# A three-branch decoder trunk: the first loads on two queues, the first piece reordered, the roots spread in two parts, the output in three pieces

## The chip, the core and the metric

The kernel runs on one core of one Trainium2 chip. Its time is what the device measures from the start to the end of one execution, in microseconds; a run's figure is the median of several executions. TensorE is called PE here, VectorE DVE, ScalarE ACT, GpSimd POOL and SyncE SP. SP does nothing here but issue transfers; ACT and POOL issue some too.

## The reference

Two layers (`DEPTH` 2) work on 256 tokens of width 1024, all in float32. Each layer normalises the stream, multiplies it by one wide matrix, feeds three token mixers, gates and adds their projections, and adds the result to the stream. A last normalisation ends the trunk.

```python
for layer in range(DEPTH):
    h = rms_norm(x, norm_w[layer])
    proj = jnp.einsum('bsd,de->bse', h, w_in[layer])       # 1024 -> 12,832 columns
    (a_xbc, a_z, a_dt, b_q, b_k, b_v, b_z,
     c_q, c_k, c_v, c_f, c_z, gates) = jnp.split(proj, split_at, axis=-1)
    y_a = mamba2_branch(...)            # state space scan
    y_b = sliding_window_branch(...)    # windowed attention with sinks
    y_c = forgetting_attention_branch(...)
    branch = jnp.einsum('bsiw,iwd->bsid', jnp.stack([y_a, y_b, y_c], axis=2), w_proj[layer])
    g = jax.nn.sigmoid(gates.reshape(b, s, 3, d) + gate_bias[layer])
    x = x + jnp.einsum('bsd,de->bse', jnp.sum(g * branch, axis=2), w_out[layer])
return rms_norm(x, final_norm_w)
```

`rms_norm` multiplies a token by the inverse root of its mean square, and each channel by a weight.

## The kernel before

**Products in three parts.** A float32 matrix is split in a high part, which has the short format that PE multiplies in one pass, and a low part, the rest. A product is high x high, low x high and high x low (`hh`, `lh`, `hl`; the letter of the tokens comes first). ACT makes the high part by a copy (`hi`), DVE the low part by a subtraction with two inputs in SBUF (`lo`).

**Weights in pieces and parts.** The weights are taken in pieces of 256 or 512 columns. A piece comes in parts of 512 KB: four blocks of 128 rows where it has 256 columns, two where it has 512. `load_part` issues the transfers of a part, and the part with number 0 comes in two halves of 256 KB. Six raw buffers (`N_RAW`) let the first six parts be asked for ahead. After these a load waits until its buffer has been split.

**The order.** In the first stage (`tc.manual_schedule` over PE, DVE, ACT and POOL) the order of each of these four engines is the order of the lines. Then only PE's order is that of the lines, and a scheduler places the other engines' work. Every engine takes its own instructions strictly in their order: an instruction that waits holds up all behind it.

**The start, line by line.** The norm weights come by ACT's queue (L183). ACT loads its function table for Exp (L186). SP's queue brings the first 128 tokens in two halves (L189), then the first weight part in two halves and the second part (L363), the second 128 tokens (L1416), the third part, the rope table (L1418), and three more parts. While PE waits it runs transposes of an identity (`WARM`, `FILL`). Then:

- `turn(t, j)` transposes half j of token block t on PE (L113), and DVE multiplies it by the norm weights (L1440) into `xw`;
- `high(t, j)` and `low(t, j)` split it (L1444, L1448);
- `w_high(part, i)` and `w_low(part, i)` split half i of a weight part (L1453, L1459);
- `hh`, `lh`, `hl` multiply four blocks of rows at a time for one token block: all of the first piece, 48 products of 256 columns (L109);
- `square(t, j)` takes sums of squares of the tokens on ACT (L244).

The tokens of the first three pieces are multiplied without their roots: the inverse roots `y0.rn` (`root` on POOL, L227, `rsqrt` on DVE, L234 to L238) are applied when ACT evicts the results (L536, L1028). The `late` list holds the evictions of the first piece.

**The normalising product.** `normalize` spreads the roots over the partitions: ACT writes a diagonal matrix for each token block (L1386), PE multiplies it by ones in plain float32, and DVE multiplies `xw` by what comes out (L1396). This product stands in PE's order after the second piece and ahead of the third. The pieces from then on:

```python
op(v, *(u_bv(y, t, first) for t in range(2)))            # first piece: multiplied already
op(None, lambda: layer_consts(y0, nc.gpsimd))
op(None, lambda: launch(9, normalize(y0), 0.0))
op(cv0, u_cv(y, 0, 0), u_cv(y, 0, 1))                    # second piece
op(cv1, u_cv(y, 256, 0), u_cv(y, 256, 1))                # third piece
```

**The end.** `out_end` adds the residual, takes sums of squares and the root for each token block, multiplies 640 columns on DVE and 384 on ACT, and sends them by SP's and ACT's queues (L1219 to L1222).

Of the kernel before, what the change touches and what calls it, by code (L numbers as in the profile page):

```python
# [14 lines left out]
ALU = mybir.AluOpType  # L15
# [20 lines left out]
FILL = 10  # L36
# [14 lines left out]
def hybrid_trunk(  # L51
# [134 lines left out]
    act(tab, tab, AF.Exp)  # L186
# [167 lines left out]
    def load_part(j):  # L354
# [5 lines left out]
        for c, ap in src:  # L360
            m = ap.shape[-1]
            for h in range(0, kper, step_):
                nc.sync.dma_start(raw[:, h:h + step_, c:c + m],  # L363
                                  ap.rearrange("(k p) c -> p k c", p=P)[:, k + h:k + h + step_, :])
# [828 lines left out]
    def out_end(y, c, t, i, n, xo, p):  # L1193
        sl = slice(c, c + n)
        with tc.high_priority():
# [19 lines left out]
            if i == 2:  # L1215
                r = row_rsqrt2(v, last)
                if last:
                    m = 640
                    ts(y.xn[:, t, 0:m], y.xn[:, t, 0:m], r[:, 0:1], None, op0=ALU.mult)  # L1219
                    nc.sync.dma_start(out2[t * P:(t + 1) * P, 0:m], y.xn[:, t, 0:m])  # L1220
                    act(y.xn[:, t, m:D], y.xn[:, t, m:D], AF.Copy, scale=r[:, 0:1])  # L1221
                    nc.scalar.dma_start(out2[t * P:(t + 1) * P, m:D], y.xn[:, t, m:D])  # L1222
# [159 lines left out]
    def normalize(y):  # L1382

        rb = T("L1", [P, S])
        for t in range(2):
            act(rb[:, t * P:(t + 1) * P], ident, AF.Copy, scale=y.rn[:, t:t + 1])  # L1386
        yield 2.0
        p = pmx()
        for t in range(2):
            mm(p[:, t * P:(t + 1) * P], ones, rb[:, t * P:(t + 1) * P], start=True, stop=True)  # L1390
# [23 lines left out]
    with tc.manual_schedule(engines={ENG.PE, ENG.DVE, ENG.Activation, ENG.Pool}):  # L1414
        load_to(2)
        nc.sync.dma_start(x0[:, 1, :], x2[P:S, :])  # L1416
        rope_sb = fin["rope"] = T("L1", [P, 2, 2, 64])
        nc.sync.dma_start(rope_sb, rope_tab.rearrange("(t p) c d -> p t c d", p=P))  # L1418
        load_to(N_RAW)
# [35 lines left out]
        def w_low(part, i):  # L1455
# [3 lines left out]
            tt(lo[:, ks, :], raw[:, ks, :], hi[:, ks, :].bitcast(F32), op=ALU.subtract)  # L1459
# [7 lines left out]
        def keys(t, k0, a, b, ends=False):  # L1467

            for k in range(k0, k0 + 4):
# [5 lines left out]
        def hh(t, k0):  # L1475
            keys(t, k0, y0.hTh, w0.hi)

        def lh(t, k0):
            keys(t, k0, y0.hTl, w0.hi)

        def hl(t, k0):
            keys(t, k0, y0.hTh, w0.lo, True)

        square(0, 0)
        turn(0, 0)
        high(0, 0)
        w_high(parts[0], 0)
# [3 lines left out]
        low(0, 0)  # L1491
        w_high(parts[0], 1)
        high(0, 1)
        w_low(parts[0], 0)
        w_low(parts[0], 1)
        w_high(parts[1], 0)
        w_high(parts[1], 1)
        low(0, 1)
        w_low(parts[1], 0)
        w_low(parts[1], 1)  # L1500
        hh(0, 0)
        lh(0, 0)
        hl(0, 0)
        hh(0, 4)
# [73 lines left out]
```

## Time and profile before

| | us |
|---|---|
| median of 3 runs | 808.71 (808.34 to 808.9) |
| the profiled execution's own time | 808.15 |
| its span, first to last instruction | 806.4 |
| PE busy | 796.9 |
| DVE busy | 684.6 |
| ACT busy | 534.0 |
| POOL busy | 171.6 |
| mean granted clock of PE | 0.999 |

The span leaves out 1.7 us around it. In a row of the timeline stand start and length in us, the engine, the line, the operation, what it writes and reads, the shapes and how many; in brackets stands how long the engine had idled before, and for what. A row of several can show overlapping instructions, so its length is not their sum. `mx` and `mm` are PSUM buffers, `L` stands for several kinds of tile, and `raw`, `hi` and `lo` for weights as loaded, their high parts and their low parts.

### The profile page before, as it was taken

The page shows a single profiled execution, that of the slowest core. Times are in us where ns is not written, and L with a number is a line of the kernel's source. Part 1 is how long each engine was busy: PE and PEld are TensorE (multiplying, and loading weights), DVE is VectorE, ACT ScalarE, POOL GpSimd, SP SyncE. Part 2 cuts the span into 40 slices and gives each one's busy share as a digit, 9 for nine tenths or more (in the row PEclk, how much of TensorE's full clock was granted, in tenths as well). Part 3 has the DMA queues.
Part 4 walks back from the last instruction along what each step waited for, and adds up shares of the span by engine and source line. Part 5 has one row for each costly group of instructions (what it writes and reads, how often), then busy time and mean ns, then how long its engine had stood idle before and what let it go on. Part 6 is the DMA issues. An engine that isn't in the chain of part 4 may idle for free.

```text
span 806.4 us, 14834 instructions
## 1 busy us (share of the span) xinstructions
PE 796.9 (99%) x5162; PEld 710.7 (88%) x5162; DVE 684.6 (85%) x1414; ACT 534.0 (66%) x1144; POOL 171.6 (21%) x238
## 2 busy tenths in 40 slices
PE   8999999999999999999999999999999999999996
PEld 7998988888888888888999899888889988888896
DVE  6869999998899997795785799999879999869865
ACT  7777767875775785543665678677747768845452
POOL 3166113130320100133001741122312120012000
PEclk9999999999999999999999999999999999999999
DMA  9998888797665566686678987679986656576632
GB/s 313 279 261 177 243 223 200 214 294 221 172 203 172 162 195 195 199 254 205 217 245 259 235 212 217 160 216 284 264 230 185 192 150 184 173 235 220 210 107 77
DMA packets 138826, 170.43 MB, mean 211 GB/s; under 512 B 9352, under 2 KB 106464, under 8 KB 138752
## 3 DMA queue, kind: packets, MB, share of 16 engines
q1 hardware_dynamic: 114960, 140.53, 56.4%
q0 software_dynamic: 13328, 13.29, 10.2%
q10 hardware_dynamic: 10464, 15.67, 6.6%
q8 instruction: 41, 0.67, 0.3%
q14 instruction: 33, 0.27, 0.1%
HBM read 154.71 MB, written 2.16 MB: 195 GB/s over the span
## 4 chain that ended last, share of the span: by engine, by line
PE 97%; DVE 1%; DMA 1%; issue 0%; ACT 0%; SPq 0%; DVEq 0%
PE mm L109 84%; PE mx L109 10%; PE mx L113 3%; DMA raw<-in_w_in_dram 1%; DVE lo L294 0%; DVE L L1097 0%; SPq L363 0%; SPq L189 0%; DVE L L1440 0%; ACT L L1444 0%; ACT hi L1453 0%; ACT L L1221 0%; DVE L L1196 0%; DVE L L1200 0%; DVE L L288 0%
## 5 line engine op out<-in xcount | busy, mean ns | idle before, releaser
L109 PE MATMUL mm<-L,hi 128*128 128x512 f32 x1056 | 354.0, 387 | 0.7 <-DVE L L1097 0.7
L294 DVE TENSOR_TENSOR lo<-raw,hi 128x1024 fp32r<-128x1024 f32 (+1 forms) x276 | 312.2, 1150 | 44.0 <-ACT hi L293 42.6
L293 ACT ACTIVATE hi<-raw 128x1024 fp32r<-128x1024 f32 (+1 forms) x276 | 265.8, 982 | 58.3 <-PE mm L109 45.2
L109 PE MATMUL mm<-hi,L 128*128 128x512 f32 (+2 forms) x1168 | 303.4, 349 | 0.1
L109 PE MATMUL mm<-L,lo 128*128 128x256 f32 x1056 | 266.6, 273 | 0.0
L109 PEld LDWEIGHTS mm<-hi,L 128*128 128x128 f32 x1168 | 205.7, 190 | 23.1 <-issue 1.7
L109 PEld LDWEIGHTS mm<-L,hi 128*128 128x128 f32 x1056 | 194.9, 190 | 27.3 <-issue 5.5
L109 PEld LDWEIGHTS mm<-L,lo 128*128 128x128 f32 x1056 | 202.1, 191 | 5.4
L109 PE MATMUL mm<-lo,L 128*128 128x512 f32 (+2 forms) x584 | 201.5, 347 | 0.0
L109 PEld LDWEIGHTS mm<-lo,L 128*128 128x128 f32 x584 | 110.2, 190 | 10.7
L491 POOL DMA_DIRECT2D L<-L x68 | 60.1, 908 | 192.8 <-ACT L L490 165.1
L1066 POOL TENSOR_SCALAR_AFFINE_SELECT bias<-bias 128x128 f32<-128x128 f32 x64 | 33.7, 559 | 76.9 <-DMA bias<-cumd 76.7
L831 DVE SCALAR_TENSOR_TENSOR L<-L,vec,L 128x255 f32<-128x255 f32 (+2 forms) x96 | 46.2, 481 | 2.0 <-ACT L L828 0.3
L489 ACT ACTIVATE L<-mm 128x256 f32<-128x256 f32 x84 | 31.8, 379 | 19.2 <-PE mm L109 14.4
L655 ACT ACTIVATE pp<-pp,nm 128x128 f32<-128x128 f32 x64 | 28.2, 442 | 23.8 <-DVE nm L649 23.8
L1100 ACT ACTIVATE L<-L 128x512 f32<-128x512 f32 x24 | 15.2, 631 | 31.4 <-DVE L L1097 27.0
L491 POOL DMA_DIRECT2D qt<-L x16 | 13.8, 860 | 76.4 <-ACT qt L490 76.4
L613 ACT ACTIVATE pp<-pp,nm 128x128 f32<-128x128 f32 x32 | 12.6, 394 | 25.6 <-DVE nm L618 24.8
L978 POOL TENSOR_TENSOR sm<-sm,mhalf 128x8 f32<-128x8 f32 x2 | 5.2, 2593 | 111.6 <-DVE sm L976 111.6
L490 ACT ACTIVATE L<-mm 128x256 f32<-128x256 f32 x68 | 26.1, 383 | 1.2 <-DMA L<-L 1.2
L1097 DVE TENSOR_TENSOR L<-mm,L 128x512 f32<-128x512 f32 x22 | 15.1, 686 | 13.6 <-PE mm L109 12.1
L1133 POOL TENSOR_TENSOR L<-L,L 128x512 f32<-128x512 f32 x8 | 12.8, 1603 | 55.4 <-DVE L L1132 49.8
(212 smaller groups left out, 925.1 us busy)
## 6 DMA issues: line engine op xcount, KB each, us to landing
raw<-in_w_in_dram SPq DMA_DIRECT2D x191, 512.0 KB, 5.1
raw<-in_w_proj_dram SPq DMA_DIRECT2D x48, 512.0 KB, 5.9
L<-L POOLq DMA_DIRECT2D x72, 128.0 KB, 5.4
raw<-in_w_out_dram SPq DMA_DIRECT2D x16, 512.0 KB, 5.2
bias<-cumd ACTq DMA_DIRECT2D x16, 256.0 KB, 3.3
L<-cumd ACTq DMA_DIRECT2D x8, 512.0 KB, 6.3
L<-in_gate_bias_dram ACTq DMA_DIRECT2D x12, 256.0 KB, 6.2
qt<-L POOLq DMA_DIRECT2D x16, 128.0 KB, 6.0
```

The lines of the kernel that those rows point to most:

```text
L109: nc.tensor.matmul(o, a, b, **kw)
L113: nc.tensor.transpose(o, a, i)
L293: keep(act)(hi, src, AF.Copy)
L294: keep(tt)(lo, src, hi.bitcast(F32), op=ALU.subtract)
L489: act(halves(lo), ordered(p[:, S:2 * S]), AF.Copy)
L490: last = act(halves(out), ordered(p[:, 0:S]), AF.Copy)
L491: nc.gpsimd.dma_start(out, lo, accum_op=ALU.add)
L655: act(pp[:, i, sl], pp[:, i, sl], AF.Exp, scale=-1.0, bias=nm[:, e:e + 1], accum_out=sums[:, e:e + 1])
L831: stt(a[:, s:S], x_[:, 0:S - s], y.vec[:, 16 * j + u:16 * j + u + 1], a[:, s:S], op0=ALU.mult, op1=ALU.add)
L1066: nc.gpsimd.affine_select(out=bias[:, i, dst], in_=bias[:, i, src], compare_op=ALU.is_ge, fill=NEG, base=0, pattern=[[-1, P]], channel_mul ...
L1097: tt(halves(g), p, halves(y.gb), op=ALU.add)
L1100: finish(act(g, g, AF.Tanh, scale=0.5))
```

## The change

- The first two weight parts go by ACT's queue. SP's queue has the tokens, then the other parts, then the rope table. The table load for Exp stands behind ACT's issues.
- In the first stage weights and tokens are split in another order, and the products of the first piece are taken in another order, some two blocks at a time. The low half of the second weight part is made by POOL (`gtt`) in place of DVE. There are three filling transposes in place of ten.
- Sums of squares come later on ACT: the second behind the split of the third part, and the last two behind the split of the fourth.
- `normalize` writes the roots as a high part (ACT) and a low part (DVE), and multiplies both by ones in the one-pass format: two products of 256 columns in place of two in plain float32.
- The evictions of the first piece come in reverse order.
- The output of each token block goes in three pieces: 352 and 352 columns by DVE and SP's queue, 320 by ACT and its queue.

```diff
@@ -33,7 +33,7 @@
 N_RAW, N_SPLIT = 6, 6
 AHEAD = 4
 WARM = 7
-FILL = 10
+FILL = 3
 D_ADD = 6.0
 EARLY = 4
 MEET = 5.0
@@ -183,7 +183,6 @@
     nc.scalar.dma_start(nw8, norm_w[0:1, :].rearrange("o (k p) -> (o k) p", p=P))
     tab = T("tab", [P, 1])
     nc.vector.memset(tab, 0.0)
-    act(tab, tab, AF.Exp)
     x0 = T("L8", [P, 2, D])
     for j in range(2):
         nc.sync.dma_start(x0[:, 0, j * 512:(j + 1) * 512], x2[0:P, j * 512:(j + 1) * 512])
@@ -360,7 +359,7 @@
         for c, ap in src:
             m = ap.shape[-1]
             for h in range(0, kper, step_):
-                nc.sync.dma_start(raw[:, h:h + step_, c:c + m],
+                (nc.scalar if j < 2 else nc.sync).dma_start(raw[:, h:h + step_, c:c + m],
                                   ap.rearrange("(k p) c -> p k c", p=P)[:, k + h:k + h + step_, :])
         raws[j] = raw
 
@@ -1215,11 +1214,13 @@
             if i == 2:
                 r = row_rsqrt2(v, last)
                 if last:
-                    m = 640
-                    ts(y.xn[:, t, 0:m], y.xn[:, t, 0:m], r[:, 0:1], None, op0=ALU.mult)
-                    nc.sync.dma_start(out2[t * P:(t + 1) * P, 0:m], y.xn[:, t, 0:m])
-                    act(y.xn[:, t, m:D], y.xn[:, t, m:D], AF.Copy, scale=r[:, 0:1])
-                    nc.scalar.dma_start(out2[t * P:(t + 1) * P, m:D], y.xn[:, t, m:D])
+                    for a, b in ((0, 352), (352, 704), (704, D)):
+                        o = y.xn[:, t, a:b]
+                        if b < D:
+                            ts(o, o, r[:, 0:1], None, op0=ALU.mult)
+                        else:
+                            act(o, o, AF.Copy, scale=r[:, 0:1])
+                        (nc.sync if b < D else nc.scalar).dma_start(out2[t * P:(t + 1) * P, a:b], o)
                 else:
                     h = layers[y.l + 1].h[t] = T("L4", [P, D])
                     for j in range(2):
@@ -1381,13 +1382,15 @@
 
     def normalize(y):
 
-        rb = T("L1", [P, S])
+        rb = [T("L1", [P, S], F32R) for _ in range(2)]
         for t in range(2):
-            act(rb[:, t * P:(t + 1) * P], ident, AF.Copy, scale=y.rn[:, t:t + 1])
+            h, l = (r[:, t * P:(t + 1) * P] for r in rb)
+            act(h, ident, AF.Copy, scale=y.rn[:, t:t + 1])
+            stt(l, ident, y.rn[:, t:t + 1], h.bitcast(F32), op0=ALU.mult, op1=ALU.subtract)
         yield 2.0
         p = pmx()
-        for t in range(2):
-            mm(p[:, t * P:(t + 1) * P], ones, rb[:, t * P:(t + 1) * P], start=True, stop=True)
+        for i in range(2):
+            mm(p[:, 0:S], onesr, rb[i], start=(i == 0), stop=(i == 1))
         both_streams(y)
         hTh, hTl = y.normal
         for k in (0, 4):
@@ -1413,10 +1416,11 @@
     ENG = mybir.EngineType
     with tc.manual_schedule(engines={ENG.PE, ENG.DVE, ENG.Activation, ENG.Pool}):
         load_to(2)
+        act(tab, tab, AF.Exp)
         nc.sync.dma_start(x0[:, 1, :], x2[P:S, :])
+        load_to(N_RAW)
         rope_sb = fin["rope"] = T("L1", [P, 2, 2, 64])
         nc.sync.dma_start(rope_sb, rope_tab.rearrange("(t p) c d -> p t c d", p=P))
-        load_to(N_RAW)
         warm = pmx()
         for i in range(WARM):
             transpose(warm[:, 0:P], ident, ident)
@@ -1452,11 +1456,11 @@
             m = raw.shape[1] // 2
             act(hi[:, i * m:i * m + m, :], raw[:, i * m:i * m + m, :], AF.Copy)
 
-        def w_low(part, i):
+        def w_low(part, i, f=tt):
             raw, hi, lo = part
             m = raw.shape[1] // 2
             ks = slice(i * m, i * m + m)
-            tt(lo[:, ks, :], raw[:, ks, :], hi[:, ks, :].bitcast(F32), op=ALU.subtract)
+            f(lo[:, ks, :], raw[:, ks, :], hi[:, ks, :].bitcast(F32), op=ALU.subtract)
 
         def square(t, j):
             sum_sq(x0, t, 512 * j, ss[:, 2 * t + j:2 * t + j + 1], 512)
@@ -1464,62 +1468,70 @@
         parts = [new_part() for _ in range(4)]
         first.extend((pmx(), pmm()))
 
-        def keys(t, k0, a, b, ends=False):
-
-            for k in range(k0, k0 + 4):
+        def keys(t, k0, n, a, b, ends=False):
+
+            for k in range(k0, k0 + n):
                 mm(first[t][:, 0:256], a[:, t, k, :], in_turn(b(k)),
                    start=(k == 0 and a is y0.hTh and not ends), stop=(k == NK - 1 and ends))
 
         w0 = pieces[0]
 
-        def hh(t, k0):
-            keys(t, k0, y0.hTh, w0.hi)
-
-        def lh(t, k0):
-            keys(t, k0, y0.hTl, w0.hi)
-
-        def hl(t, k0):
-            keys(t, k0, y0.hTh, w0.lo, True)
+        def hh(t, k0, n=4):
+            keys(t, k0, n, y0.hTh, w0.hi)
+
+        def lh(t, k0, n=4):
+            keys(t, k0, n, y0.hTl, w0.hi)
+
+        def hl(t, k0, n=4):
+            keys(t, k0, n, y0.hTh, w0.lo, True)
 
         square(0, 0)
         turn(0, 0)
+        w_high(parts[0], 0)
+        w_low(parts[0], 0)
         high(0, 0)
-        w_high(parts[0], 0)
+        low(0, 0)
         turn(0, 1)
         for i in range(FILL):
             transpose(warm[:, 0:P], ident, ident)
-        low(0, 0)
         w_high(parts[0], 1)
+        w_low(parts[0], 1)
         high(0, 1)
-        w_low(parts[0], 0)
-        w_low(parts[0], 1)
-        w_high(parts[1], 0)
-        w_high(parts[1], 1)
         low(0, 1)
-        w_low(parts[1], 0)
-        w_low(parts[1], 1)
-        hh(0, 0)
-        lh(0, 0)
-        hl(0, 0)
-        hh(0, 4)
+        hh(0, 0, 2)
+        hl(0, 0, 2)
+        lh(0, 0, 2)
+        hh(0, 2, 2)
+        lh(0, 2, 2)
+        hl(0, 2, 2)
         turn(1, 0)
         turn(1, 1)
-        lh(0, 4)
-        square(0, 1)
+        w_high(parts[1], 0)
+        w_low(parts[1], 0, gtt)
         high(1, 0)
+        low(1, 0)
+        w_high(parts[1], 1)
+        w_low(parts[1], 1, gtt)
         high(1, 1)
-        low(1, 0)
         low(1, 1)
-        hl(0, 4)
+        hh(0, 4, 2)
+        lh(0, 4, 2)
         hh(1, 0)
+        hl(1, 0)
         lh(1, 0)
-        hl(1, 0)
+        hh(0, 6, 2)
+        lh(0, 6, 2)
         hh(1, 4)
         lh(1, 4)
+        hl(0, 4)
         hl(1, 4)
         for i in range(2):
             w_high(parts[2], i)
             w_low(parts[2], i)
+        square(0, 1)
+        for i in range(2):
+            w_high(parts[3], i)
+            w_low(parts[3], i)
         square(1, 0)
         square(1, 1)
         v = T("sm", [P, 8])
@@ -1527,10 +1539,6 @@
                                 op=ALU.add)
         ts(v[:, 0:2], v[:, 0:2], 1.0 / D, EPS, op0=ALU.mult, op1=ALU.add)
         r0 = root(v, 2)
-        for part in parts[3:]:
-            for i in range(2):
-                w_high(part, i)
-                w_low(part, i)
         y0.rn = rsqrt(v, 2, r0)
 
         for i, f, _ in ops[:2]:
@@ -1539,7 +1547,7 @@
         release(pieces[0], 2)
         run_op(*ops[2])
     with tc.manual_schedule(engines={ENG.PE}):
-        for g in late:
+        for g in reversed(late):
             g()
         for i, f, last in ops[3:]:
             run_op(i, f, last)
```

## The prediction

> **What bounds the kernel now.** I read the page first: is any engine full, and what does the last chain consist of.
>
> ```profile
> PE 796.9 (99%) x5162; PEld 710.7 (88%) x5162; DVE 684.6 (85%) x1414; ACT 534.0 (66%) x1144; POOL 171.6 (21%) x238
> PE 97%; DVE 1%; DMA 1%; issue 0%; ACT 0%; SPq 0%; DVEq 0%
> ```
>
> PE holds 97% of the chain. The change leaves the PE work from the third weight piece to the last output product as it is, so only the two ends can give or cost anything: what passes before PE runs without a break, and what follows its last product. A microsecond won at the start comes out at the end, because nothing between idles to absorb it. So next I read the chain of waits in its first 22 us (start, length, what), and the timeline row of the product that follows the normalisation, which I use as the finishing post of the start.
>
> ```profile
> 2.71 5.90 DMA raw<-in_w_in_dram
> ...
> 12.94 7.86 PE mm L109 x68
> 20.80 0.45 PE mx L109 x4
> ```
> ```profile
> 21.00 0.47 PE L109 MATMUL mm<-hi,L 128*128 128x256 f32 x2
> ```
>
> The start hangs on one transfer: the second weight part (512 KB, issued at 2.71) lands at 8.61. After 12.94 PE never stops: 68 products in 7.86 us, 0.116 us each, then the normalising product, 0.45 us, then the post at 21.00. The question is when the post comes after the change. Third, the DMA view of the first 4.2 us and the timeline of the issues there, since the change reorders these.
>
> ```profile
> raw<-in_w_in_dram SPq DMA_DIRECT2D x2, 512.0 KB, 6.8
> L<-in_x_dram SPq DMA_DIRECT2D x2, 256.0 KB, 2.9
> raw<-in_w_in_dram SPq DMA_DIRECT2D x2, 256.0 KB, 4.4
> L<-in_x_dram SPq DMA_DIRECT2D x1, 512.0 KB, 6.7
> ```
> ```profile
> 0.81 0.59 ACTq L183 DMA_DIRECT2D L<-in_norm_w_dram  x1
> 0.81 0.87 SPq L189 DMA_DIRECT2D L<-in_x_dram  x2
> ...
> 1.73 1.45 SPq L363 DMA_DIRECT2D raw<-in_w_in_dram  x3
> ...
> 3.22 0.51 SPq L1416 DMA_DIRECT2D L<-in_x_dram  x1
> ```
>
> One issue costs about 0.45 us of its engine. The second tokens, issued at 3.22, land at 3.22+6.7=9.9. The two 512 KB weight parts average 6.8 us to landing; one took 5.9, so the other, issued at 3.77 when the tokens' issue ended, took 7.7 and landed at 11.5. In order of arrival, then: 1536 KB by 8.6, 2048 KB by 9.9, 2560 KB by 11.5; 1.3 to 1.6 us for each 512 KB. The start is fed by bytes, not by issues.
>
> ```profile
> GB/s 0 0 16 211 302 324 251 284 321 313 362 354 385 388 368 366 346 342 347 347 347 351 347 364 377 382 383 410 364 383 328 349 255 165 219 284 284 252 227 227
> ```
>
> This is the DMA view of 0 to 25 us, a slice being 0.625 us: from 2.5 to 6.25 us it moves about 300 GB/s, later 350 to 385. So at best a fuller early queue saves 3.75 x (1 - 300/360) = 0.6 us.
>
> **The change part by part: when the second weight part lands.** ScalarE's queue now has the norm weights (0.81), the two halves of the first part (1.4 and 1.85) and the second part (about 2.3). SyncE has the first tokens (0.81, 1.25), the second tokens (1.7) and the third weight part (2.2). Ahead of the second part lie the first part, the first tokens and now the second tokens too, 1536 KB, and the third part is issued beside it. Its landing, which I call T, is therefore 9.9 when it goes ahead of the third part and 11.5 when it goes behind it; with the 0.6 us of a fuller queue, 9.3 and 10.9; and if tokens and weights shared by bytes and it passed the tokens, near 8.6 less 0.6, 8.0, where the second tokens bind instead. How the two queues share is what before does not show at its start; the nearest row is a transfer issued on ScalarE's queue at 23.6, beside weights from SyncE:
>
> ```profile
> L<-in_gate_bias_dram ACTq DMA_DIRECT2D x1, 256.0 KB, 6.1
> ```
> ```profile
> bias<-cumd ACTq DMA_DIRECT2D x16, 256.0 KB, 3.3
> ```
>
> The first row took 6.1 us, the second kind, the same size and mostly on empty queues, 3.3: being on the other queue did not let it pass what was ahead. So I go by order of issue, between 9.3 and 10.9: T=10.1. The unknown's ends for the range are 8.9 and 11.5.
>
> **From T to the post, path of PE.** Durations:
>
> ```profile
> 8.63 1.15 ACT L1453 ACTIVATE hi<-raw 128x512 fp32r<-128x512 f32 x2 [0.62 <-DMA raw<-in_w_in_dram]
> ```
> ```profile
> 14.32 0.61 ACT L244 ACTIVATE L<-L 128x512 f32<-128x512 f32 x1
> ```
> ```profile
> 17.49 2.36 DVE L294 TENSOR_TENSOR lo<-raw,hi 128x1024 fp32r<-128x1024 f32 x2
> ```
>
> The high half of the second part takes ScalarE 0.6 us, so PE's next product is at T+0.7. Before T it has done the 12 products of the first part with the first tokens and, if these have landed, the eight transposes of the second tokens. Left are 36 products of the first piece and 48 of the second: 84 x 0.116 = 9.7, so T+10.4 with no wait between.
>
> There is one: the low half of the second part moves from VectorE to GpSimd, which takes
>
> ```profile
> 732.20 1.28 POOL L1133 TENSOR_TENSOR L<-L,L 128x512 f32<-128x512 f32 x1 [13.26 <-DVE L L1132]
> ```
> ```profile
> 338.15 2.13 POOL L1133 TENSOR_TENSOR L<-L,L 128x512 f32<-128x512 f32 x1 [14.53 <-DVE L L1132]
> ```
> ```profile
> 339.68 1.69 DVE L294 TENSOR_TENSOR lo<-raw,hi 128x1024 fp32r<-128x1024 f32 x1
> ```
>
> 1.28 us undisturbed, but 2.13 where VectorE's two-input subtraction ran beside it, and that subtraction took 1.69 for the 1.2 of its peers: they take turns. Two such operations run from T+0.7, and exactly then VectorE has the two token subtractions, which PE wants at about T+2.1 and gets about T+2.7 (0.6 late), and the second GpSimd half ends 0.3 to 0.5 us after PE could use it. I take 1.0 us of waits, between 0 (no turns) and 1.5: T+11.4. The Trainium skill, "SBUF — State Buffer", section "SBUF: two separate sides", says that VectorE with two SBUF inputs and GpSimd exclude each other on a shared port pair for a whole instruction. The stretched rows agree with it; were there no such lock, PE's path would be the T+10.4.
>
> **From T to the post, path of the roots.** The normalising product needs the row sums of squares, and behind it in PE's queue stands all that follows. The sums move back on ScalarE: after T come eight splits (0.53 each, two in 1.15 with overlap) and three squares (0.61), 6.1 us with the read-out 6.25; before, only one split pair and two squares stood between the last token split and the sums. The root and its refinement:
>
> ```profile
> 15.05 0.16 DVE L1526 TENSOR_REDUCE sm<-ss 128x2 f32<-128x4 f32 x1 [0.37 <-ACT L L244]
> ```
> ```profile
> 15.57 0.72 POOL L227 TENSOR_TENSOR sm<-sm,mhalf 128x2 f32<-128x2 f32 x1 [12.22 <-DVE sm L1528]
> ```
> ```profile
> 17.41 0.16 DVE L238 TENSOR_TENSOR rs<-sm,sm 128x2 f32<-128x2 f32 x1
> ```
>
> 15.05 to 17.57 is 2.5 us, of which 0.5 was spent behind a subtraction that now comes earlier: 2.0, T+8.3. The new low part of the spread root is two VectorE operations, and they are queued behind two 1024-wide subtractions (2.36): T+10.6; the two cost 0.15 to 0.4 each, T+11.1. The two normalising products now run at 0.116 each instead of 0.45 together, so 0.2 us less on PE: post at T+11.4 by this path, T+11.6 by PE's. Both paths meet; I take T+11.5 = 21.6, that is **+0.6 us** against 21.00. With T=8.9, 20.4 (-0.6); with T=11.5, 23.0 (+2.0).
>
> **At no cost.** Seven filling transposes less (0.11 each): PE waits there for weights anyway. Three more issues on ScalarE delay its table load and first square by 1.4 us; its first split waits for weights until over 5 us. The rope table goes behind three weight parts on SyncE; it is used after the post. The reversed evictions move 0.36 us between two buffers that the third piece needs only at the post.
>
> **The end.**
>
> ```profile
> 802.17 0.62 ACT L1221 ACTIVATE L<-L,rs 128x384 f32<-128x384 f32 x1 [0.68 <-DVE rs L264]
> 802.17 0.55 DVE L1219 TENSOR_SCALAR L<-L,rs 128x640 f32<-128x640 f32 x1
> 802.75 0.36 SPq L1220 DMA_DIRECT2D out_dram<-L  x1
> 802.82 0.36 ACTq L1222 DMA_DIRECT2D out_dram<-L  x1
> ```
> ```profile
> out_dram<-L SPq DMA_DIRECT2D x1, 320.0 KB, 2.5
> out_dram<-L ACTq DMA_DIRECT2D x1, 192.0 KB, 2.7
> ```
>
> The last landing is 802.82+2.7=805.5. After: VectorE's first 352 columns take 0.30 (by width) to 0.4 and go at 802.55, the second go at about 802.9, ScalarE's 320 at 802.74. The first bytes start 0.2 earlier, the last issue is 0.1 later but smaller: -0.2, between -0.35 and +0.1.
>
> **Sum.** 0.6-0.2=+0.4 on the profiled run's 808.15 (span 806.4 and 1.7 around it) gives 808.55. That run lies 0.56 under the median 808.71; on the median +0.4 gives **809.1**. A difference under 0.2% (1.6 us) is about what a measurement of this kernel cannot tell from none.
>
> **Rivals.** *Faster: fuller, fair queues.* T=8.0 and second tokens at 8: post at T+11.5=19.5, -1.5, and -0.35 at the end: 806.9. For it: the early slices at 300 GB/s. Against: the same transfers compete, and tokens and weights cannot both be early. Chance 0.10 for all over 0.2% faster.
>
> *Slower: the second weights arrive last.* Place: ScalarE's queue at the start. If tokens, with 2 and 4 KB rows, win over weights with 1 KB rows, or issue order puts the third part first without a fuller queue, T=11.5, post 23.0: 808.71+2.0-0.2 = 810.5, up to 811 with 0.5 more of turns. It decides from T=11.1 on. Chance 0.19. The Trainium skill, "DMA: Bandwidth & Descriptors", section "Issuing engines are not separate DMA queues", says that several issuing engines save only issue time and share the same engines; by that rule there is no fuller queue, T lies in 9.9 to 11.5. The 6.1 us row agrees.
>
> *Slower: PE's clock falls back.*
>
> ```profile
> 3.76 1.79 PE L113 MATMUL mx<-ident,L 128*128 128x128 f32 x7
> ```
> ```profile
> 5.38 1.25 PE L113 MATMUL mx<-ident 128*128 128x128 f32 x10
> ```
>
> PE's first transposes come at about 0.21 us, those from 5.38 on at 0.11: it starts at half pace. Between the first 12 products and T+0.7 PE now idles some 2 us with fewer filling transposes. If that returns it to half pace for the 3.8 us from 1.54 to 5.4 that it first took, 1.9 us are lost: 811. Chance 0.03.
>
> **Numbers.** Forecast, within 0.2%: 0.68. Faster 0.10, slower 0.19+0.03=0.22. The range reaches from T=8.9 with the best end, 808.71-0.6-0.35 = 807.8, less 0.2 for the spread of a run, 807.5, to T=11.5 with extra turns, 811.0.
>
> **What would show it.** After: the second part's landing (ScalarE's first wait for it) near 10.1 and behind or beside the second tokens; GpSimd's two subtractions well over 1.28; a wait of PE at the normalising product on VectorE or none over 0.5; the post near 21.6; the last issue at 802.9 shifted with it. I am wrong if the second part lands before 9, if sums of squares end before T+5.5, or if a wait appears after 40 us that before does not have.

## The result, and the profile after

| | us |
|---|---|
| forecast | 809.1 (807.5 to 811.0) |
| median after, 7 runs | 810.84 (809.67 to 811.71) |
| median before, 7 runs | 808.62 (807.85 to 808.9) |
| ratio | 1.0029, 95% interval 1.0019 to 1.0039 |
| after, profiled execution: own time, span | 809.67, 808.0 |

The kernel is 2.2 us slower: inside the range, but not the case held likeliest (within 0.2%). It is the case of the rival "the second weights arrive last", given 0.19. The profiled execution is the quickest of the seven, so its lines show the smallest loss; the next section has a second profile.

PE still holds the chain (page, total busy time and chain by engine). PE's busy time is 0.1 us less, and the span 1.6 us more: the loss is idle time of PE.

```profile
PE 796.8 (99%) x5153; PEld 710.8 (88%) x5153; DVE 686.6 (85%) x1416; ACT 533.9 (66%) x1144; POOL 175.5 (22%) x240
PE 96%; DVE 2%; DMA 1%; issue 1%; ACTq 0%; ACT 0%; POOL 0%; DVEq 0%; POOLq 0%
```

The chain of waits of the first 26 us (start, length, what):

```profile
2.39 8.40 DMA raw<-in_w_in_dram
10.79 0.02 issue
10.81 0.63 ACT hi L1457
11.44 0.53 ACT L L1448
...
11.99 1.08 DVE L L1452
...
13.29 0.83 DVE L L1452
...
14.98 2.48 DVE lo L1463 x4
...
17.87 0.73 POOL sm L226
...
20.55 0.92 DVE lo L293
...
21.68 0.62 DVE L L1389 x2
22.30 0.04 issue
22.34 0.38 PE mx L109
```

The second weight part, issued at 2.39 on ACT's queue, lands at T=10.79 where before it landed at 8.61. From there the chain goes over splits on ACT, the token subtractions and then the weights' low halves on DVE, the root on POOL, and the roots' low part behind 1024-wide subtractions on DVE. The prediction laid out all but one of these stations: it let the sums wait for the last square, which ends at 16.93, but DVE's low halves of the weights held them until 17.46. The post in the timeline:

```profile
21.91 0.82 PE L109 MATMUL mx<-L,ones 128*128 128x256 f32 x2
22.57 0.38 PE L109 MATMUL mm<-hi,L 128*128 128x256 f32 x2
```

22.57 against 21.00: the start lost 1.57 us. Why T is late stands in the issues (timeline) and the DMA view of 0 to 13 us:

```profile
1.73 0.42 SPq L1420 DMA_DIRECT2D L<-in_x_dram  x1
2.20 2.37 SPq L362 DMA_DIRECT2D raw<-in_w_in_dram  x3
```
```profile
1.43 1.45 ACTq L362 DMA_DIRECT2D raw<-in_w_in_dram  x3
```
```profile
raw<-in_w_in_dram ACTq DMA_DIRECT2D x2, 256.0 KB, 5.3
L<-in_x_dram SPq DMA_DIRECT2D x1, 512.0 KB, 5.1
raw<-in_w_in_dram ACTq DMA_DIRECT2D x1, 512.0 KB, 8.4
```

The second tokens (512 KB), issued at 1.73, land at 6.88: earlier than the second half of the first weight part, issued 0.15 later (7.78), and 3.1 us earlier than before. The third part lands at 10.46, before the second at 10.79. By bytes the queue is fuller, 2560 KB by 10.79 against 11.47; but the bytes that came early are the second tokens and the third part, which the first piece uses last or not at all. How the queues shared can be counted from the packets of the trace: from 5 to 6 us, with second tokens (rows of 4 KB) on SP's queue, that queue moved 336 to 369 GB/s and ACT's (rows of 1 KB) 16 to 74; from 7 to 9.5 us both carried rows of 1 KB, and each moved some 170 to 200.

At the end, the last product of each kernel (before, then after), and the issues of the output after:

```profile
799.85 0.28 PE L109 MATMUL mm<-lo,L 128*128 128x256 f32 x1
```
```profile
801.10 0.28 PE L109 MATMUL mm<-lo,L 128*128 128x256 f32 x1
...
803.84 0.81 SPq L1223 DMA_DIRECT2D out_dram<-L  x2
804.00 0.34 ACTq L1223 DMA_DIRECT2D out_dram<-L  x1
```

The last product ends at 800.13 and 801.37: of the 1.57 us 1.25 arrive. A wait of PE for DVE (L1097, 0.42 us at 151 us before) is gone and took in 0.27. From there to the end of the program it is 6.31 us before and 6.60 after.

### The profile page after: what moved, and what is told of

Its sections match the earlier page's. It is cut to its first block, busy times and chain, and to the rows that moved or that the text cites. A ratio compares the mean times of both kernels' runs of the same rounds, so it can differ in the third digit from the quotient of the medians.

```text
span 808.0 us, 14827 instructions
## 1 busy us (share of the span) xinstructions
PE 796.8 (99%) x5153; PEld 710.8 (88%) x5153; DVE 686.6 (85%) x1416; ACT 533.9 (66%) x1144; POOL 175.5 (22%) x240
## 4 chain that ended last, share of the span: by engine, by line
PE 96%; DVE 2%; DMA 1%; issue 1%; ACTq 0%; ACT 0%; POOL 0%; DVEq 0%; POOLq 0%
PE mm L109 83%; PE mx L109 9%; PE mx L113 3%; DMA raw<-in_w_in_dram 1%; DVE lo L293 0%; DVE lo L1463 0%; DVE L L1452 0%; DVE L L1096 0%; ACTq L362 0%; POOL sm L226 0%; ACT hi L1457 0%; DVE L L1389 0%; ACTq L183 0%; ACT L L1448 0%; DVE L L1195 0%
## 5 line engine op out<-in xcount | busy, mean ns | idle before, releaser
L836 ACT ACTIVATE L<-L 128x256 f32<-128x256 f32 x32 | 13.4, 418 | 17.0 <-DVE L L830 16.9
```

## The experiments

Theory A: the loss is the late weights of the first two parts on ACT's queue, and work that stands behind them. Theory B: the roots' path sets the post whatever T is. Theory C: the three output pieces cost 0.3. Theory D came up with the first profiles below: PE works at half pace for longer.

In the table, T, w0b (second half of the first part) and x1 (second tokens) are landings; "pace" is when PE's products begin to follow each other at 0.11 instead of 0.21 us. All from one profile each; medians from the timed runs, to be compared with the kernel before on the same chip, as the ratio is: 808.62 for after, 808.52 for the next four, 808.24 for dve_low to before_fill3, 808.26 for one_queue.

| kernel | w0b | x1 | T | pace | post | median | ratio, 95% |
|---|---|---|---|---|---|---|---|
| before | 6.83 | 9.94 | 8.61 | 5.4 | 21.00 | 808.62 | |
| after | 7.78 | 6.88 | 10.79 | 8.6 | 22.57 | 810.84 | 1.0019 to 1.0039 |
| after_again | 8.80 | 7.49 | 11.27 | 11.4 | 23.36 | 810.91 | 1.0019 to 1.0042 |
| q_undo | 6.60 | 9.68 | 8.34 | 9.9 | 22.06 | 810.28 | 1.0013 to 1.0032 |
| q_only | 8.58 | 7.62 | 11.61 | 7.4 | 24.00 | 811.42 | 1.0027 to 1.0052 |
| tail_undo | 8.81 | 7.65 | 11.82 | 13.2 | 24.46 | 811.46 | 1.0021 to 1.0046 |
| dve_low | 7.99 | 7.20 | 11.00 | 11.1 | 23.04 | 810.98 | 1.0023 to 1.0048 |
| fill10 | 8.07 | 6.82 | 11.08 | 8.4 | 22.86 | 811.17 | 1.0022 to 1.0049 |
| one_part | 9.23 | 7.73 | 12.25 | 15.4 | 24.29 | 811.12 | 1.0022 to 1.0048 |
| tokens_act | 7.74 | 7.60 | 9.25 | 9.9 | 22.05 | 809.42 | 1.0005 to 1.0024 |
| best_a | 7.73 | 6.15 | 9.16 | 7.5 | 20.38 | 809.38 | 1.0003 to 1.0020 |
| best_b | 8.23 | 8.17 | 9.52 | 9.5 | 21.41 | 809.10 | 0.9998 to 1.0015 |
| before_fill3 | 6.75 | 10.45 | 9.08 | 10.5 | 21.47 | 808.75 | 0.9997 to 1.0015 |
| one_queue | 7.11 | 8.50 | 9.99 | 5.9 | 20.55 | 808.51 | 0.9993 to 1.0011 |

**after_again**: no edit.

> The changed kernel once more, unaltered, for a second profile. Its first profile had the second weight part landing at T=10.79, the post (first product after the normalising one) at 22.57, and the last landing followed by 1.3 us to the end of the program; its times ran from 809.67 to 811.71. Theory A (the loss hangs on T, and T depends on how the two queues happen to share): the second profile has another T, and the post again at T+11.8 within 0.3. A profile with T near 11.5 has the post near 23.2 and a time near 811. Theory B (the roots set the post whatever T is): the post stays at 22.4 to 22.8 even if T moves by 0.5 or more, and the spread of the times comes from a later place. Median of the timed runs: 810.5 to 811.0 under both.

T=11.27, post 23.36, span 809.0 for the same program. Of the 1.0 us between the two spans, 0.79 lies ahead of the post. The chain of waits starts elsewhere this time:

```profile
1.88 6.92 DMA raw<-in_w_in_dram
...
9.50 1.65 PE mx L109 x6
11.15 0.62 PE mx L113 x4
...
11.79 0.70 DVE L L1444
...
12.52 0.63 ACT L L1448
...
16.91 1.23 ACT L L243 x4
```

Now the second half of the first part, landing at 8.80, is the late one. PE's products of it stand ahead of the second tokens' transposes (first product at 9.50, last transposes from 11.15), so tokens that landed at 7.49 are first split at 12.52. From there ACT's splits and squares (L243) lead to the roots, and PE waits for their low part:

```profile
22.44 0.28 PE L109 MATMUL mx<-L,ones 128*128 128x256 f32 x1
23.14 0.39 PE L109 MATMUL mx<-L,ones 128*128 128x256 f32 x1 [0.42 <-DVE L L1389]
```

Theory A holds in that the arrivals set the post, and T+12.09 is just inside "T+11.8 within 0.3"; but T is not the only late arrival that counts. The chain also holds PE's products at half pace (six in 1.65 us). Part of B holds too: the roots' path is the last by 0.4 us. In all seven profiles with these queues T lies between 10.79 and 12.25, and the third part has landed before the second.

**q_undo** and **q_only**: the queues alone, taken out of the change (shown; the order of SP's issues goes back too) and, with the order of issues and the place of the table load, put into the kernel before.

```diff
-                (nc.scalar if j < 2 else nc.sync).dma_start(raw[:, h:h + step_, c:c + m],
+                nc.sync.dma_start(raw[:, h:h + step_, c:c + m],
```

> The changed kernel with all its early loads back on SyncE's queue in the order of before; the order of work, GpSimd's low halves, the two-part roots and the three output pieces stay. Theory A: T returns to about 8.6 to 9.1, second tokens land at 9.9. Laying out each engine's queue with the durations of the two traces, ScalarE then waits for the second tokens at 9.9 behind the first half of the second part, token splits start at 11.3, and the post comes at about 22.0: 0.6 us earlier than in the changed kernel, still 1.0 later than before. Time 0.5 to 1.0 us under the changed kernel, about 810.0. Theory B (roots set the post): the squares end at 16.3 as they did at 16.9, post 22.0 too, but then GpSimd's halves and T have no part in it; told apart by the run with VectorE's low halves. A theory by which only the queues cost would put the post back at 21.0 and the time at 808.9 with the end's 0.3.

> The kernel before with one thing of the change: the first part's two halves and the second part go by ScalarE's queue, then the tables of ScalarE, and SyncE's queue has first tokens, second tokens, third part and on, rope table last. Order of work as before. Theory A: T about 10.8, second tokens at 6.9; work written for second weights first and tokens later stalls on both, post 22.7 to 23.1 against 21.0, time 810.4 to 811.0 (the end stays as before). Theory B: the squares end at 16.4 instead of 15.0, post 22.4. If the queues cost nothing, post 21.0 to 21.3 and 808.7 to 809.

The queues alone (q_only) cost 2.9 us, more than the whole change and more than expected. This run shows the cause most plainly, since all work stands in the order of before: T is 3.00 later than before (11.61), the post 3.00 later (24.00), the last product 2.90 later, and the median 2.90.

```profile
2.40 9.21 DMA raw<-in_w_in_dram
...
15.94 7.86 PE mm L109 x68
```
```profile
24.00 0.47 PE L109 MATMUL mm<-hi,L 128*128 128x256 f32 x2
```

Whether the new order of work gets some of it back is not shown: the changed kernel's median is 0.5 to 0.6 lower, within the spread of the times, and with the old output (tail_undo, below) it is the same as q_only's. Without the queues (q_undo) 0.6 us of the changed kernel's loss goes, also within the spread, and 1.8 stays, with the post at 22.06 as laid out. The two do not add up to the change's 2.2, because both hold up the same post. In q_undo the chain hangs on the second tokens, which are last again and now have more behind them:

```profile
3.21 6.48 DMA L<-in_x_dram
...
11.22 0.63 ACT L L1448
...
21.84 0.39 PE mx L109
```

ACT's order alternates the halves of the second part with those of the second tokens, so ACT waits for the tokens with half of the second part unsplit, and squares and roots come after. The order suits neither arrival: the one of before, where tokens are last, nor its own, where weights are last.

**tail_undo**: the output in two pieces again.

```diff
-                    for a, b in ((0, 352), (352, 704), (704, D)):
...
+                    m = 640
+                    ts(y.xn[:, t, 0:m], y.xn[:, t, 0:m], r[:, 0:1], None, op0=ALU.mult)
...
```

> The changed kernel with the output in its old two pieces (640 columns on SyncE, 384 on ScalarE). Theory C: the last landing comes 0.08 us later against the last product than with three pieces, but the end of the program follows it by 0.96 us instead of 1.33, so 0.3 us less: median about 810.5. The prediction's step (three pieces win 0.2) would give 811.0. The start is the changed kernel's: post 22.3 to 23.0.

Its median, 811.46, misses both expectations and says nothing on the end, since the times spread by 1.6 us with the start (T=11.82 in the profile). The profiles do: from the end of the last product to the end of the program it is 6.59 to 6.62 us in all seven with three pieces, and 6.30 to 6.32 in all seven with two. Theory C is shown: three pieces cost 0.29. The reason was read from the semaphore events of the trace and not tried by itself: the last landing is 0.08 us earlier against the last product (5.27 instead of 5.35 us), but SP, which ends the program by going through the transfers' semaphores at some 0.06 us each, has the semaphore of the transfer that lands last (SP's second piece) first in its order and the rest still ahead of it.

**dve_low**, **fill10** and **one_part**: one part of the changed start undone in each.

```diff
-        w_low(parts[1], 0, gtt)
+        w_low(parts[1], 0)
...
-        w_low(parts[1], 1, gtt)
+        w_low(parts[1], 1)
```
```diff
-FILL = 3
+FILL = 10
```
```diff
-        rb = [T("L1", [P, S], F32R) for _ in range(2)]
+        rb = T("L1", [P, S])
...
-        for i in range(2):
-            mm(p[:, 0:S], onesr, rb[i], start=(i == 0), stop=(i == 1))
+        for t in range(2):
+            mm(p[:, t * P:(t + 1) * P], ones, rb[:, t * P:(t + 1) * P], start=True, stop=True)
```

> The changed kernel with the two low halves of the second weight part back on VectorE; all else as changed. Theory A (late landings, made worse by GpSimd and VectorE taking turns): VectorE's two token subtractions return from 1.37 to 1.77 us to about 0.69 each, the squares end no earlier (they are ScalarE's), but the first-piece products no longer wait for the token subtractions: with T as in the first profile (10.8) the post is at 22.0 instead of 22.57, with T near 11.5 at 22.9 to 23.3. Post at T+11.2 to T+11.6 as against T+11.8 to T+12.6; time 0.2 to 0.6 under the changed kernel, about 810.4. Theory D (TensorE's pace: with three filling transposes it stays at 0.21 us a product until 8.6, 11.4 or 13.2 us, where before it went to 0.11 at 5.4): no change where TensorE reaches its full pace late, since the token work then waits for the transposes.

> The changed kernel with ten filling transposes again instead of three, all else as changed. In the three profiles of the changed start TensorE's products came every 0.21 us until 8.6, 11.4 and 13.2 us, the later the longer the profile's start; before, with ten, every 0.11 us from 5.4 us. Theory D (the half pace costs time): full pace from 5.4 to 9 us, the 12 products of the first part in 1.4 instead of 1.7 to 2.6 us, the second tokens' eight transposes in 0.9 instead of 1.7; where the second half of the first part lands at 8.8 this brings the post 0.3 to 0.6 earlier (T+11.8 to T+12.1 always), the spread of the times shrinks, and the median falls by 0.2 to 0.5 to about 810.5. Theory A alone: TensorE waits for T in any case, post and time unchanged within 0.2.

> The changed kernel with the roots spread in one part as before (no low part, four normalising products of 128 columns in fp32). In the profiles of the changed kernel TensorE waits 0.3 to 0.6 us at its second normalising product for the low part, which VectorE computes behind two 1024-wide subtractions. If that wait is on the path: from the first normalising product to the post 0.37 instead of 0.66 to 0.91, post and time 0.1 to 0.5 earlier; the roots themselves then bind if they are late (their last spread on ScalarE ends 21.4 in the first profile against TensorE's 21.9, so they do not). Theory A: a gain of at most 0.5, and the rest of the loss, at least 1.5 us, remains. Theory B (the roots are the bound): the post follows the spread by 0.6 and the gain is 0.3 or more.

None brought the gain that was expected of it. Their medians, 810.98, 811.17 and 811.12, are 2.7 to 2.9 over before on the same chip, where the change is 2.2 and 2.4 over it; the intervals overlap. dve_low's post, T+12.04, missed its forecast of T+11.2 to T+11.6 too. POOL's and DVE's operations in the changed kernel, then DVE's in dve_low:

```profile
11.53 2.98 POOL L1463 TENSOR_TENSOR lo<-raw,hi 128x512 fp32r<-128x512 f32 x2 [8.17 <-ACT hi L1457]
```
```profile
11.99 3.06 DVE L1452 TENSOR_TENSOR L<-L,L 128x512 fp32r<-128x512 f32 x2 [0.46 <-ACT L L1448]
```
```profile
13.27 0.68 DVE L1452 TENSOR_TENSOR L<-L,L 128x512 fp32r<-128x512 f32 x1
...
14.48 0.69 DVE L1452 TENSOR_TENSOR L<-L,L 128x512 fp32r<-128x512 f32 x1
```

Two subtractions in 3.06 us beside POOL, 0.69 each without: the turns are real. But in dve_low's profile PE was at half pace until 11.1, its tokens came late for that reason, and the post was at T+12.04. With ten fills the pace came at 8.4, and the chain is that of the first profile, turns and low part included: T+11.78 again.

With the roots in one part the wait of 0.1 to 0.4 us at the normalising product is gone. But PE came to full pace only at 15.4, and from its first product at 9.23 to the post it has no wait at all (chain of waits):

```profile
8.03 0.63 ACT hi L1455
...
9.23 2.93 PE mx L109 x12
12.16 1.71 PE mx L113 x8
...
18.28 5.81 PE mm L109 x52
```

In this execution T=12.25 held up nothing. The first weight half, landing at 8.01, and the half pace set the post; the eight products from 13.5 to 15.4 alone took some 0.9 us longer than at 0.11 each. In after_again, dve_low and tail_undo, too, the chain goes from a late half of the first part through products at half pace, and not through T. Their posts and one_part's are at T+12.04 to T+12.64, where the two profiles with the changed order whose chain goes through T have T+11.78. So a late first part and half pace together cost 0.3 to 0.9 us more than T alone would; they were not taken apart. To undo one of turns, pace and low part uncovers the next. What undoing all three would give with the changed queues was not run.

**tokens_act**: the queues exchanged.

```diff
-        nc.sync.dma_start(x0[:, 0, j * 512:(j + 1) * 512], x2[0:P, j * 512:(j + 1) * 512])
+        (nc.scalar if j else nc.sync).dma_start(x0[:, 0, j * 512:(j + 1) * 512], x2[0:P, j * 512:(j + 1) * 512])
...
-                (nc.scalar if j < 2 else nc.sync).dma_start(raw[:, h:h + step_, c:c + m],
+                nc.sync.dma_start(raw[:, h:h + step_, c:c + m],
...
-        nc.sync.dma_start(x0[:, 1, :], x2[P:S, :])
+        nc.scalar.dma_start(x0[:, 1, :], x2[P:S, :])
```

> The changed kernel with the queues exchanged: SyncE has the first half of the first tokens, then all weights in order; ScalarE has the norm weights, the second half of the first tokens and the second tokens. Work order, GpSimd's halves, roots, three fills and three output pieces stay. Theory A (two queues share about one to one, tokens with their larger rows ahead; what is lost is the order among the weights): the weights of the first two parts no longer share with the third part, which is behind them on their own queue, so T comes at 8.9 to 9.6, the first part at 5.2 and 6.4 to 6.9, the second tokens at 6.8 to 8.0, 2 MB in all by 9.6 as against 9.9 before and 10.8 after. Post 20.9 to 21.5, time about 809.0 to 809.6. If the bytes shared evenly without regard to rows, second tokens 9 and T 9.5. A rival by which more than one queue costs bandwidth gives T over 10 and no gain.

T=9.25 and 809.42, as forecast: 1.2 us over before on the same chip instead of 2.2 to 2.4, with nothing but the queues exchanged. With all weights on one queue the third part no longer competes with the second (10.76 for the third). The second tokens, now on ACT's queue and issued 0.12 later than the second half of the first part, again landed ahead of it (7.60 and 7.74); from 5.5 to 6.5 us they moved 319 to 336 GB/s by the trace's packets, and SP's weights 61 to 64. So the longer rows went ahead on either queue. That their length is the reason is argued: no run changed it. The post, 22.05, missed its forecast of 20.9 to 21.5: PE was at half pace until 9.9 (12 products in 2.80 us) and PE waited for the roots' low part.

```profile
7.23 2.80 PE mx L109 x12
10.02 0.45 PE mx L113 x4
```

**before_fill3**: the kernel before with `FILL = 3`.

> The kernel before with three filling transposes instead of ten, nothing else. Theory D (TensorE's half pace costs time by itself): full pace comes at 8 to 10 us instead of 5.4, 20 products and eight transposes of the first part run at 0.21 instead of 0.11, and the post comes 0.5 to 1.5 later, time 808.8 to 809.8. Theory A: TensorE waits for the second part at 9.3 and for second tokens at 9.8 and 12.2 in any case; the slower products fit in front of these waits, post within 0.25 of 21.0 unless the pace changes after 10 us, time within 0.3 of before.

Its pace changed at 10.5 and its post came 0.47 later, but its second part and second tokens had landed 0.47 and 0.51 later too. The median, +0.5, has an interval that holds no change. The profiles say more: before, q_only and before_fill3 have the same order of work and changed pace at 5.4, 7.4 and 10.5, and in all three the post comes 12.39 us after T. So the half pace cost nothing there by itself, and the later landings make up the whole 0.47.

**best_a**, **best_b**, **one_queue**: the first piece in order of arrival, with DVE's low halves, one-part roots, ten fills and two output pieces. best_a has the first tokens and all weights on SP's queue and the second tokens on ACT's; best_b has tokens_act's queues; one_queue has everything on SP's queue with the second tokens ahead of the second part. The loads of best_a and of one_queue against the changed kernel's, and the head of one_queue's order of work:

```diff
-        load_to(2)
-        act(tab, tab, AF.Exp)
-        nc.sync.dma_start(x0[:, 1, :], x2[P:S, :])
+        load_to(2)                                       # best_a; all weights by nc.sync
+        nc.scalar.dma_start(x0[:, 1, :], x2[P:S, :])
+        act(tab, tab, AF.Exp)
```
```diff
+        act(tab, tab, AF.Exp)
+        load_to(1)                                       # one_queue; all weights by nc.sync
+        nc.sync.dma_start(x0[:, 1, :], x2[P:S, :])
...
+        turn(0, 0)
+        turn(0, 1)
+        high(0, 0)
...
+        turn(1, 0)
+        turn(1, 1)
+        hl(0, 2, 2)
+        lh(0, 0, 2)
...
```

> A version built on what the runs so far showed: SyncE has the first tokens and then all weights in order, ScalarE only the norm weights and the second tokens (512 KB) beside them; the first piece's work stands in the order in which the bytes then come (both halves of the first tokens on VectorE and TensorE ahead of the weights' low halves, second tokens' transposes ahead of most products of the first part, first-part products of both token blocks ahead of the second part's); low halves on VectorE, roots in one part, ten fills, output in two pieces. Theory A (arrival order of the weights and work queued behind late bytes make the loss): landings first tokens 3.6 and 4.6 to 4.8, first part 5.8 to 6.5 and 6.8 to 7.6, second tokens 6.9 to 8.2, T 8.8 to 9.2, third part 10.5; laying the queues out with the traces' durations gives the post at 19.8 to 20.7 as against 21.0 before, and a time 0.3 to 1.2 us under the kernel before: 807.2 to 808.1. If a second queue always costs more at the start than it brings, the post is over 21.5 and the time over 809.

> As the version with all weights on SyncE behind the first tokens, but with the queues of the run that exchanged them: the second half of the first tokens goes by ScalarE's queue too, so the first weight half is issued 0.45 earlier. Landings as there: first tokens 3.8 and 5.4, first part 5.0 and 7.7, second tokens 7.6, T 9.25. Laid out with these, post 20.2 to 21.0 and a time of 0 to 0.8 us under the kernel before. Theory A: work queued in order of arrival takes away most of the 1.2 us that the exchanged queues alone still cost, that is post at least 1.0 under their 22.05. If instead the roots bound that run, post stays over 21.7.

> A version with one queue: all early loads on SyncE as before, but the second tokens ahead of the second weight part (first tokens, first part in two halves, second tokens, second part, third part, rope table after the sixth part), and the first piece's work in that order, the row sums and their root a little ahead of the last low half so that ScalarE's work behind the root is not late; low halves on VectorE, roots in one part, ten fills, two output pieces. In the versions with two queues the post came at 20.38 and 21.41, yet the last product ended at 800.18 and 800.93, that is 0.4 to 0.7 us of the start's gain came back as waits at 29, 151 and 547 us; the one at 29 us is set by the end of the root, which was 0.43 later than before. Theory A (transfers on two queues let single packets of the first weights come late, differently in each run; on one queue they come in order): first part 5.3 to 5.9 and 6.6 to 6.8, second tokens 8.3 to 9.1, T 9.7 to 10.4, spread of the times about 1.0 us as before, not 1.6 to 2. Laying the queues out with the traces' durations: post at 20.2 to 21.0, 0.3 to 0.4 under before for the same landings, root at 17.5; time between 0.4 under before and equal. If the order of work itself cost time, as it does in the changed kernel with its loads back on one queue (1.8 us over before), it is over 809.2.

best_a's post, 20.38, is 0.62 earlier than before and within the forecast, yet its last product ends at 800.18, 0.05 later, and its median missed the forecast by over 1 us. The shift against before goes from -0.62 to -0.14 around this wait, which before does not have (PE's waits of 26 to 32 us, and the chain up to it):

```profile
PE mm L109 <- DVE lo L293: 0.2, 1, 0.2
```
```profile
17.85 0.17 DVE rs L237
...
19.78 1.07 ACT hi L292
...
28.03 1.15 DVE lo L293
29.17 0.04 issue
29.22 0.48 PE mm L109
```

The end of the roots (18.01; 17.58 before) starts ACT's evictions, behind them the third piece's splits, and then DVE's normalised tokens and the next low half, which PE needs at 29 us. A wait for DVE at 547 us took the rest (0.6 us there, 0.2 before). one_queue shows the same: post 0.45 earlier, 0.36 of it back at 29 us, median 808.51 and no difference. Its landings are in order and its times spread 1.3 us (807.85 to 809.19), where the changed kernel's spread 2.0; but before_fill3's, on one queue too, spread 1.8, so the spread proves little. No version beats the kernel before. best_b missed its forecast in post (21.41) and time; its last product ends 0.80 later than before, and its median is 0.86 over, with an interval that just holds no change. best_a's is of its quickest execution, 1.2 under its median; what the slower ones lose was not profiled.

## Why the prediction was right and where it failed

- **When the second weight part lands: too early by 0.7 to 1.2 us.** "By order of issue, T=10.1" failed; "behind or beside the second tokens" was right. The tokens were not merely ahead: they passed the first part's second half, and then the third part shared with the second to the end. The bounds 8.9 and 11.5 held the first two profiles; three of the seven with these queues were over 11.5. By the rule that the prediction took from the Trainium skill, "DMA: Bandwidth & Descriptors", section "Issuing engines are not separate DMA queues", T was 9.9 to 11.5: the measured 10.79 and 11.27 agree, though the first profile had its 2560 KB 0.7 us sooner than one queue.
- **The rival's point.** "From T=11.1 on" it was to be slower; T of the two profiles of the change lies on both sides. The rival's sum, 810.5 to 811 for T=11.5, is what the median came to. The error was to give 0.68 to a T in the middle between two transfers that race, where the rows on ACT's queue were known to be the shorter ones. The range held because this T was taken as its upper end, and the median lies near that end.
- **From T to the post: T+11.5 forecast, T+11.78 and T+12.09 measured.** Both paths do meet within 0.4 us. In the first profile the path runs from T, with 0.5 us more in front of the sums (DVE's low halves); in the second it starts at the first part's late half, which the prediction left out. POOL's turns came as laid out: its halves took 1.29 and 1.74 us and DVE's 1.37 and 1.77 instead of 0.69. They depend on what meets: in after_again POOL took 1.27 and 1.29, DVE 0.69 and 1.36. The rule of the Trainium skill, "SBUF — State Buffer", section "SBUF: two separate sides", agrees with these times, and with dve_low, where each takes 0.69.
- **"At no cost: seven filling transposes less"** failed as a reason: PE did not only wait there, it also came to full pace later. What the prediction feared (PE falling back, 0.03) was not the case, it rose late. The size is nothing in the order of before (T+12.39 in three profiles) and, together with a late first part, 0.3 to 0.9 us in the changed order.
- **"Nothing between idles to absorb it"** failed in both directions. A loss of 1.57 lost 0.3 on its way, and a gain of 0.62 in best_a came back whole: the post is not the only finish, the roots' end is a second one, some 0.4 us behind before's.
- **The end: -0.2 forecast, +0.29 measured.** The issues and landings were about right (-0.08); what follows the last landing was not looked at.

The sum with measured terms: for the first profile 1.57-0.32+0.29=1.54 against a span 1.53 longer; for the second 2.36-0.12+0.29=2.53 against 2.53. The median's 2.2 lies between. So the forecast of +0.4 missed 1.3 in the start (of which T is 0.7 to 1.2 and the rest T to post, less what was absorbed), and 0.5 at the end.

## What to carry to other kernels

Two queues at a kernel's start are a race: cost each transfer between "alone" and "last", and take the late end where its rows are the shorter ones (here rows of 1 KB lost to rows of 4 KB on either queue); weights that are used in order belong on one queue. Where an engine's order interleaves data of two transfers, any late byte holds the whole order, so the order must follow arrivals that are measured and stable. A gain at the start counts only up to the next late consumer; look for the second finish before adding it to the sum.

## What was not expected of the hardware

- **Single late packets.** In tail_undo, of the sixteen shares of the first weight half, one for each DMA engine, fourteen had come by 6.60 and the last two at 7.86; in the first profile fifteen by 5.48 and one at 6.05. In the seven profiles with these queues the last of the sixteen came 0.03 to 2.01 us behind the fourteenth, in the four with all early loads on one queue 0.08 to 0.56. It is a likely source of the start's spread; no run isolates it.
- **A granted clock of 1.00 without a record.** Windows of PE (stretch, length, busy and products, granted clock, DMA share, GB/s), tail_undo and then before:

```profile
10.00:12.00 2.00, 2.00 (x11) 1.00 1.09 350
```
```profile
14.00:16.00 2.00, 2.00 (x20) 1.00 1.08 368
```

  Fully busy in both, 11 instructions against 20, and the clock column reads 1.00 in both. But the trace's clock records begin only where full pace begins, at 13.15 us in tail_undo, 5.33 before and 15.39 in one_part, and the view counts a stretch without a record as 1.00. So the column says nothing of PE's first microseconds; the distance of the products does. These first records last 791.9, 795.3 or 798.7 us, so their lengths differ by steps of 3.41 us. The Trainium skill, "TensorE: Matmul & The Clock Gate", section "Part 1: The HAM clock gate (the "warmup" mystery)", says that PE runs at half rate until a free-running window of about 3.4 us was busy. The steps agree with it, and so do the changes at 5.4 to 9.5 us with ten fills and at 8.6 to 15.4 with three, the latest behind the longest idle stretches (2.9 and 2.8 us in tail_undo and one_part).
- **The end of a program has an order of its own**: 0.96 us after the last landing with two output pieces, 1.33 with three.
